# Tying every instruction of a planned decoder step to its written order on all five queues

## The chip, the cores and the metric

The kernel runs on one core of one Trainium2 chip. The core has five instruction queues: PE (TensorE, matrix multiplication; the profile shows its weight loads as PEld), DVE (VectorE), ACT (ScalarE), POOL (GpSimd) and SP (SyncE, which here issues all DMAs). Each queue is worked off in its order; an instruction that waits for a semaphore holds up what stands behind it. The metric is the device time of one execution in microseconds (us), the median of several runs. Lower is better.

## The reference

One layer of a hybrid decoder for 16 meta tokens, a prompt of 256 tokens and 8 x 4 sample tokens, 304 columns in all, in float32. Cut to what matters:

```
xn = rms_norm(x, norm_mix)
z = xn @ w_in                                  # 2048 -> 3360 + 4096 columns
o_a, S_a = rwkv7_mixer(z[:, :3360], ...)       # 16 heads of 64: a recurrence with state S
o_b, S_b = retention_mixer(z[:, 3360:], ...)   # 4 heads of 256: chunkwise retention
h = x + concat(o_a, o_b) @ w_out               # 2048 -> 2048
hn = rms_norm(h, norm_ffn)
h = h + (silu(hn @ w_gate) * (hn @ w_up)) @ w_down   # 2048 -> 5632 -> 2048
y = rms_norm(h, norm_final)
```

It returns y for prompt and samples, the last row of z of each sequence (the token shift), and the new states.

## The kernel before

**The main stream.** All weights lie in one array, `big`, in the order of their use: the input projection (59 tiles of up to 128 columns), the output projection in two halves of 16 tiles, and then, four hidden tiles at a time, gate, up and down. `main` (L608) walks through it. A weight is wanted as the sum of two float32r parts, so for every 512 columns, called a half here, ACT casts the raw weights to `wh` (`cast`, L591) and DVE takes the rest into `wl` (`rest`, L603). The activations are split in the same way into `xh` and `xl`. Each step of `main` issues three matmuls into an accumulator `acc`: wh by xh, wh by xl, wl by xh. Raw weights come in loads of 1024 columns, 512 KB, into one of four buffers `wr` (`load`, L582); `wh` and `wl` have four buffers each (`WS = 4`), `acc` has two banks of PSUM, and the other six banks serve the small matmuls (tag `mm`). At the start of a half, `main` writes loads up to four chunks of 1024 columns ahead, and casts so that the half two places on is cast; `rest` for that one is written in the middle of the half:

```
while self.loaded < min(total, at + WR * WCOLS):
    self.load()
while self.halved < min(total, at + (1 if starting else WS - 1) * 512):
    self.cast()
...
if o == 256:
    self.rest()
```

**The streams.** All other work is written as generators, called streams here: the evacuation of an accumulator (`evacuate`, L653), the eight pairs of RWKV heads (`pair`, L880, with `by_token`, `inverse`, `units`, `sample` and `pair_out`), the four retention heads (`ret`, L1353), norms and gates. A stream issues some instructions and yields. `inverse` (L1069) has a chain on POOL: three groups of ten small operations, each behind five shuffles on DVE that bring its factors; the ten operations of a group and the five shuffles of the next are written together, and then the stream yields. `ret` loads the samples' states, `s0r`, in four transfers of 512 KB, two at a time. `prep` in `out_jobs` (L1593) splits eight tiles of the mixers' output at once (an ACT copy and a DVE subtraction for each), before each half of the output projection. `hn` (L673) does the same for the input of the feed-forward part; at the last tile of the output projection eight of them are written in a row. `need` of a job holds `main` back until what it reads has been issued.

**The order of the work.** The program is built twice. The first build is a draft in a throw-away program. There each instruction goes through `Timed` (L289) to `Plan.book` (L345), which keeps a clock for each engine and works out, from the places in memory that an instruction reads and writes and from written-in prices, when it starts and when its result can be used. `Plan.run` (L438) lets `main` go on by one step, or a stream whose time has come: `pick` (L421) takes the first stream, by rank, whose last instructions are all done by PE's clock, and `step` (L430) lets it issue up to its next yield and sets its time to the end of these plus 100 ns. Each choice is put into `log`. Then `Room.place` (L469) lays the tiles of the draft out in one arena per data type, two tiles in one place where their uses in the written order don't meet. The second build takes its choices from `log` and makes the same instructions in the same order. Outputs are kept in `self.outs` and are written to the program at least 20 us of PE's clock later (`put`, L539; `flush`, L543). The last statements of `build` (L1671) are the write of the token shift, `out_sh`, and a last flush:

```
self.plan.run(self.main(jobs))
self.sp.dma_start(self.O["sh"], self.shout)
self.flush(all=True)
```

**What happens to that order.** The second build runs in a `TileContext`. It finds which instruction depends on which, adds the semaphores, and puts the instructions of each engine into an order of its own; the order in which they were written is for it a rank among those that it takes to be ready. So in the kernel before, the written order is a wish and not what stands in the queues.

## Time and profile before

| | us |
|---|---|
| median of 3 runs | 1605.94 |
| lowest and highest | 1604.27, 1607.81 |
| the profiled execution | 1606.78 |
| its span, from the first to the last instruction | 1605.0 |

The rows of the profile are from the one profiled execution. Nearly every instruction carries L300, the line of `call` in `Timed`, so groups are told apart by their tiles: `acc<-xh,wl` is a matmul of `main` that reads the rest of a weight, `wh<-wr` a cast, `mm<-...` a small matmul of a stream, and `arena_dt.float` any tile of the float32 arena. A group's row has its number of instructions, busy time, mean duration of one in ns, and then the idle time of its engine before it with what ended that. A row of the waits has who waited for whom, us in total, times, and the longest. A row of the timeline has start and duration in us, and in brackets the idle time before it and what ended it. A row of the windows has the length of the stretch, busy us (and instructions) of PE, PEld, DVE, ACT and POOL, the granted clock of PE as a share of full, the share of DMA time, and GB/s. The stages by their tiles: the input projection with the mixers beside it to some 640 us, the output projection after it, the feed-forward part to some 1590 us, and the last norm.

### The profile page before, as it was taken

The page shows a single profiled execution, that of the slowest core. Times are in us where ns is not written, and L with a number is a line of the kernel's source. Part 1 is how long each engine was busy: PE and PEld are TensorE (multiplying, and loading weights), DVE is VectorE, ACT ScalarE, POOL GpSimd, SP SyncE. Part 2 cuts the span into 40 slices and gives each one's busy share as a digit, 9 for nine tenths or more (in the row PEclk, how much of TensorE's full clock was granted, in tenths as well). Part 3 has the DMA queues.
Part 4 walks back from the last instruction along what each step waited for, and adds up shares of the span by engine and source line. Part 5 has one row for each costly group of instructions (what it writes and reads, how often), then busy time and mean ns, then how long its engine had stood idle before and what let it go on. Part 6 is the DMA issues. An engine that isn't in the chain of part 4 may idle for free.

```text
span 1605.0 us, 31012 instructions
## 1 busy us (share of the span) xinstructions
PE 1552.0 (97%) x11388; PEld 1518.1 (95%) x11388; DVE 1125.4 (70%) x2590; ACT 841.2 (52%) x1795; POOL 186.5 (12%) x567
## 2 busy tenths in 40 slices
PE   9998899988998999999999999999999999999997
PEld 8988898887997899999999999999999999999997
DVE  7988778886897759767565656565666666565657
ACT  6756676746775565456444444444444444444445
POOL 1454323422141300000000000000000000000000
PEclk9999999999999999999999999999999999999998
DMA  8443333334445347755555555555555555555553
GB/s 278 147 126 99 106 111 113 110 114 147 140 139 172 91 154 239 239 166 161 168 162 167 171 161 169 170 162 168 168 163 169 166 164 170 164 165 171 163 167 112
DMA packets 77001, 252.50 MB, mean 157 GB/s; under 512 B 9393, under 2 KB 14641, under 8 KB 76849
## 3 DMA queue, kind: packets, MB, share of 16 engines
q1 hardware_dynamic: 76848, 250.52, 50.4%
q8 instruction: 90, 1.47, 0.4%
q14 instruction: 63, 0.51, 0.1%
HBM read 236.21 MB, written 14.28 MB: 156 GB/s over the span
## 4 chain that ended last, share of the span: by engine, by line
PE 66%; DVE 1%; ACT 0%; issue 0%; POOL 0%; DVEq 0%; POOLq 0%
PE acc L300 63%; PE mm L300 3%; DVE arena_dt.float L300 1%; ACT arena_dt.float L300 0%; DVE wl L300 0%; POOL arena_dt.float L300 0%; DVEq L1740 0%; ACT wh L300 0%; DVEq L300 0%; POOLq L300 0%
## 5 line engine op out<-in xcount | busy, mean ns | idle before, releaser
L300 ACT CAST wh<-wr 128x512 fp32r<-128x512 f32 x826 | 510.4, 620 | 585.6 <-PE acc L300 549.8
L300 PE MATMUL acc<-xh,wh 128*128 128x288 f32 (+2 forms) x2592 | 793.3, 306 | 0.0
L300 PE MATMUL acc<-xh,wl 128*128 128x288 f32 (+2 forms) x2592 | 773.7, 299 | 6.5 <-DVE wl L300 6.5
L300 PE MATMUL acc<-xl,wh 128*128 128x288 f32 (+2 forms) x2592 | 770.9, 297 | 0.0
L300 DVE TENSOR_TENSOR wl<-wr,wh 128x512 fp32r<-128x512 f32 x826 | 570.5, 692 | 280.0 <-ACT wh L300 256.5
L300 PEld LDWEIGHTS acc<-xh,wl 128*128 128x128 f32 x2592 | 489.5, 189 | 8.7 <-DVE wl L300 7.2
L300 PEld LDWEIGHTS acc<-xh,wh 128*128 128x128 f32 x2592 | 491.0, 189 | 4.9 <-issue 1.9
L300 PEld LDWEIGHTS acc<-xl,wh 128*128 128x128 f32 x2592 | 490.0, 189 | 3.5 <-issue 0.2
L300 PE MATMUL acc<-arena_dt.float32r,wh 128*128 128x288 f32 x1408 | 279.9, 294 | 0.0
L300 PEld LDWEIGHTS acc<-arena_dt.float32r,wh 128*128 128x128 f32 x1408 | 226.3, 188 | 0.3 <-ACT arena_dt.float32r L300 0.3
L300 PE MATMUL acc<-arena_dt.float32r,wl 128*128 128x288 f32 x704 | 207.9, 295 | 0.0
L300 PE MATMUL mm<-arena_dt.float 128*128 128x128 f32 (+6 forms) x1072 | 175.3, 320 | 31.5 <-DVE arena_dt.float L300 13.3
L300 PEld LDWEIGHTS mm<-arena_dt.float 128*128 128x128 f32 (+1 forms) x1072 | 141.6, 185 | 48.3 <-issue 18.8
L300 DVE TENSOR_TENSOR arena_dt.float<-arena_dt.float 128x288 f32<-128x288 f32 (+11 forms) x483 | 158.0, 354 | 11.7 <-ACT arena_dt.float L300 6.2
L300 DVE TENSOR_TENSOR arena_dt.float<-arena_dt.float,acc 128x288 f32<-128x288 f32 x208 | 94.3, 454 | 64.2 <-PE acc L300 64.1
L300 PEld LDWEIGHTS acc<-arena_dt.float32r,wl 128*128 128x128 f32 x704 | 132.3, 188 | 0.0
L300 ACT COPY arena_dt.float<-mm 64x64 f32<-64x64 f32 (+9 forms) x330 | 91.8, 287 | 57.9 <-PE mm L300 52.3
L300 ACT ACTIVATE arena_dt.float<-arena_dt.float 128x288 f32<-128x288 f32 (+6 forms) x200 | 85.5, 432 | 49.5 <-DVE arena_dt.float L300 37.7
L300 DVE TENSOR_TENSOR arena_dt.float<-acc,arena_dt.float 128x288 f32<-128x288 f32 (+4 forms) x181 | 72.9, 420 | 31.3 <-PE acc L300 30.5
L300 POOL TENSOR_TENSOR arena_dt.float<-arena_dt.float 128x75 f32<-128x75 f32 (+14 forms) x240 | 81.4, 339 | 61.1 <-DVE arena_dt.float L300 36.7
L300 POOL COPY arena_dt.float<-arena_dt.float 128x32 f32<-128x32 f32 (+4 forms) x123 | 45.3, 384 | 102.0 <-DVE arena_dt.float L300 49.4
L300 POOL MEMSET arena_dt.float<- 128x64 f32 (+8 forms) x137 | 30.9, 238 | 184.4 <-DVE arena_dt.float L300 82.3
(64 smaller groups left out, 693.3 us busy)
## 6 DMA issues: line engine op xcount, KB each, us to landing
wr<-big SPq DMA_DIRECT2D x409, 512.0 KB, 3.5
arena_dt.float<-s0r SPq DMA_DIRECT2D x16, 512.0 KB, 4.6
out_rts<-arena_dt.float SPq DMA_DIRECT2D x16, 512.0 KB, 2.8
arena_dt.float<-xT SPq DMA_DIRECT2D x4, 576.0 KB, 4.7
out_y<-arena_dt.float SPq DMA_DIRECT2D x8, 288.0 KB, 2.2
arena_dt.float<-xT SPq DMA_DIRECT2D x7, 304.0 KB, 5.6
wr<-big SPq DMA_DIRECT2D x8, 256.0 KB, 5.5
arena_dt.float<-lora SPq DMA_DIRECT2D x16, 128.0 KB, 2.3
```

The costliest lines, as they stand in the source:

```text
L300: return f(*a, **k)
```

## The change

The kernel hands `Plan` a function `keep`. In the second build it is `tc.keep_in_program_order`, in the draft it does nothing. `Timed` passes each instruction through it. For an instruction it looks for the one written last on the same engine and adds an edge between the two that fixes their order in the queue and adds no semaphore. As each engine of the kernel is reached through `Timed`, and SP's DMAs too, all five queues then hold their instructions in the order in which they were written.

```diff
@@ class Timed
         def call(*a, **k):
             self._plan.book(self._name, what, a, k)
-            return f(*a, **k)
+            return self._plan.keep(f(*a, **k))
@@ class Plan
-    def __init__(self, nc, rooms, draft, log):
+    def __init__(self, nc, rooms, draft, log, keep):
+        self.keep = keep
         self.rooms, self.draft, self.log, self.count = rooms, draft, log, 0
@@ class Step
-        self.plan = pl = Plan(self.nc, rooms, draft, log)
+        self.plan = pl = Plan(self.nc, rooms, draft, log, (lambda i: i) if draft else tc.keep_in_program_order)
```

## The prediction

> **What bounds the kernel now.** I read the page first: shares, then slices.

> ```profile
> span 1605.0 us, 31012 instructions
> PE 1552.0 (97%) x11388; PEld 1518.1 (95%) x11388; DVE 1125.4 (70%) x2590; ACT 841.2 (52%) x1795; POOL 186.5 (12%) x567
> PE   9998899988998999999999999999999999999997
> DVE  7988778886897759767565656565666666565657
> ```

> PE is the bound, and each slice is 40.1 us, so all the eights lie in the first 13, before 525 us. The windows view by stage says how much is open:

> ```profile
> core 0: us, PE busy (x) PEld busy (x) DVE busy (x) ACT busy (x) POOL busy (x), PEclk, DMA share, GB/s
> 60.00:600.00 540.00, 499.92 (x3506) 472.12 (x3505) 426.62 (x1326) 342.25 (x906) 171.38 (x515) 0.97 0.41 125
> 600.00:640.00 40.00, 40.00 (x283) 39.24 (x283) 37.81 (x85) 22.16 (x47) 0.00 (x0) 1.00 0.70 231
> 640.00:1580.00 940.00, 939.97 (x7104) 937.57 (x7104) 594.79 (x1038) 424.81 (x741) 0.00 (x0) 1.00 0.55 169
> 1580.00:1605.00 25.00, 14.51 (x110) 14.07 (x108) 16.66 (x37) 9.62 (x19) 0.00 (x0) 0.78 0.24 95
> ```

> From 640 us on PE is never idle, its clock is full, and 7104 matmuls in 939.97 us are 132 ns each: no order can shorten that. What can move lies in 60 to 600: 540 - 499.92 = 40.1 us idle, and a granted clock of 0.97, worth 0.03 x 540 = 16 us. The pot is 56 us. The waits view of PE for that stretch says who ends the idle time (39.6 us together):

> ```profile
> PE mm L300 <- DVE arena_dt.float L300: 13.3, 7, 4.7
> PE mm L300 <- ACT arena_dt.float L300: 11.1, 12, 3.9
> PE mm L300 <- DMA arena_dt.float<-s0r: 8.7, 3, 6.8
> PE acc L300 <- DVE wl L300: 6.5, 3, 3.3
> ```

> These are few, long waits at the head of PE's queue. To see what an order has to do with them I took two in the timeline. The first is the wait for wl at 91 us (PE, then DVE, then POOL):

> ```profile
> 94.45 0.41 PE L300 MATMUL acc<-xh,wl 128*128 128x304 f32 x1 [3.28 <-DVE wl L300]
> ...
> 89.63 0.01 DVE L300 LOAD_MASK_SELECT arena_dt.float<-arena_dt.float  x1 [2.10 <-POOL arena_dt.float L300]
> 91.73 0.01 DVE L300 LOAD_MASK_SELECT arena_dt.float<-arena_dt.float  x1 [0.43 <-POOL arena_dt.float L300]
> 93.69 0.71 DVE L300 TENSOR_TENSOR wl<-wr,wh 128x512 fp32r<-128x512 f32 x1
> ...
> 85.17 10.87 POOL L300 TENSOR_TENSOR arena_dt.float<-arena_dt.float 128x75 f32<-128x75 f32 x26
> ```

> POOL is in the chain of `inverse`. DVE stands with a shuffle at its head, waiting for POOL, and the wl that PE needs is queued behind it. The second is the longest wait, 6.8 us for s0r (SP, POOL, PE):

> ```profile
> 480.59 0.34 SPq L300 DMA_DIRECT2D out_sh<-shout  x1
> 481.02 0.89 SPq L300 DMA_DIRECT2D arena_dt.float<-s0r  x2
> ...
> 480.00 0.56 POOL L300 COPY shout<-arena_dt.float 128x1 f32<-128x1 f32 x2
> ...
> 487.07 2.04 PE L300 MATMUL mm<-arena_dt.float 128*32 128x256 f32 x16 [6.79 <-DMA arena_dt.float<-s0r]
> ```

> The write of out_sh is the last but one statement of build, yet here it goes at 480.6 us. SP issued it as soon as POOL's copies into shout were through, with two loads of s0r right behind it, and PE waited for one of these. So today's order isn't the order of the code, and it puts instructions ahead of their inputs on in-order queues.

> **The change, part by part.** It adds no arithmetic, no transfer and no semaphore wait of its own: each instruction is tied behind the one written before it on its engine. What moves is the order on PE, DVE, ACT, POOL and SP. The written order is made by the draft: `pick` lets a stream go on when the draft's PE clock has reached the end of all that the stream last issued. So it is as good as the draft's prices. I check these against rows:

> ```profile
> L300 ACT CAST wh<-wr 128x512 fp32r<-128x512 f32 x826 | 510.4, 620 | 585.6 <-PE acc L300 549.8
> L300 DVE TENSOR_TENSOR wl<-wr,wh 128x512 fp32r<-128x512 f32 x826 | 570.5, 692 | 280.0 <-ACT wh L300 256.5
> wr<-big SPq DMA_DIRECT2D x409, 512.0 KB, 3.5
> arena_dt.float<-s0r SPq DMA_DIRECT2D x16, 512.0 KB, 4.6
> ```

> Cast: 108 + 0.83 x 512 + 94 = 627 ns against 620. Rest: 62 + 1.05 x 512 + 83 = 683 against 692. Matmul of 288 columns: 0.417 x 288 + 13 = 133 against 132. POOL at 75 elements: 260 + 2.4 x 75 = 440, and 60 + 30 more where one needs the other's output, against 10.87 / 26 = 418. A 512 KB load: 1.4 + 1.64 + 0.6 = 3.6 us against 3.5 for wr and 4.6 for s0r. The prices hold within a few per cent, are long on POOL and 1 us short on s0r. So:

> 1. PE's waits for DVE and ACT, 24.4 us. A small matmul is written where its inputs are due, with weight matmuls ahead of it. An input late by 0.2 us costs 0.2 us, not 4. I leave 5 of 24.4: -19.4. Bounds: 0 left, or all 24.4.
> 2. Wait for s0r, 8.7 us. out_sh goes to the end, and the long one of 6.8 goes; the other 1.9 stays, as s0r is priced short: -6.8.
> 3. Wait for wl, 6.5 us. In the written order DVE gets the second and third group of shuffles only when POOL's ten operations before are due, so it doesn't stand before POOL: -6.5.
> 4. **What comes back.** The cast of half h+2 is written at the start of half h, its rest in the middle of half h, 1.5 halves = 18 matmuls = 2.4 us before its use. With 0.69 for the operation itself, 1.7 us are left; now a cast may run until its four buffers are full. A burst over 1.7 us on DVE, or one over 2 us on ACT, then reaches PE, since casts and rests are queued behind it. Three bursts are plain in the code: twice eight copies and rests in `prep`, and the eight `hn` at the last out tile. This row gives 0.40 us for one:

> ```profile
> 84.32 0.80 ACT L300 ACTIVATE arena_dt.float<-arena_dt.float 128x288 f32<-128x288 f32 x2
> ```

>    Eight are 3.2 us, the lead of a cast is two halves, 3.2 us, and then come the cast and the rest, 1.3 us: 1.3 to 1.5 us of PE each, 4 in all. Smaller pile-ups, where two pairs, a sample and an evacuation come at once, I put at 0.5 us for each of 8 pairs and 4 heads, 6 us. Together +10. Bounds: 0, and the second rival's 65.
> 5. Clock. 16 us are lost after waits. These rows are of the stretches behind the wait at 94.45 and behind two more, whose rows stand below them:

> ```profile
> 94.00:100.00 6.00, 5.54 (x29) 5.55 (x30) 6.00 (x16) 1.97 (x4) 3.56 (x10) 0.72 0.29 105
> 347.00:353.00 6.00, 5.16 (x27) 4.85 (x27) 2.53 (x5) 2.27 (x7) 0.56 (x2) 0.72 0.24 87
> 379.00:385.00 6.00, 4.70 (x34) 4.47 (x35) 5.56 (x16) 2.73 (x7) 0.38 (x1) 1.00 0.55 155
> ...
> 347.84 1.64 PE L300 MATMUL mm<-arena_dt.float 128*128 128x128 f32 x8 [2.25 <-DVE arena_dt.float L300]
> 379.65 0.41 PE L300 MATMUL acc<-xh,wl 128*128 128x304 f32 x1 [2.41 <-DVE wl L300]
> ```

>    The first two fall to 0.72, the third doesn't, so two waits of one length cost different amounts, and I scale with idle time: 39.6 - 32.7 + 10 = 17 us left of 40, thus 7 of 16 us: -9. [...]
> 6. The end. out_sh now stands behind the eight writes of y: one more issue, +0.5 us. The first 20 us and all from 640 to 1580 I cost at nothing: there PE is fed by casts and rests alone, DVE is 63% busy (594.79 / 940), and the 1.7 us above cover one evacuation. If that cover fails, rival two decides.

> Sum: -19.4 - 6.8 - 6.5 + 10 - 9 + 0.5 = -31. The profiled execution took 1606.8 us (span 1605.0 and 1.8 around it), so it becomes 1575.6; the median before, 1605.9, is 0.8 lower: **1575**.

> [...]

> **Rivals.**
> - **Only what is plainly out of order pays.** The draft is slower than the chip at each hand-over: a stream waits 100 ns and then for the next group of three matmuls, 0.4 us. Then the chains of the pairs lag, `need` blocks the main stream, and PE waits as long elsewhere. For: POOL's price is long. Against: almost every long wait now has weight matmuls right behind it, so PE had work. Only out_sh's 6.8 us and its stretch at half clock, 3.4 us, go: 1606 - 10 = 1596.
> - **Slower: casts late.** In the strict order every wait of DVE at the head of its queue passes to the rest behind it. The waits view for 60 to 600:

> ```profile
> DVE arena_dt.float L300 <- PE mm L300: 41.4, 38, 6.1
> DVE arena_dt.float L300 <- POOL arena_dt.float L300: 28.5, 30, 3.1
> DVE wl L300 <- ACT wh L300: 23.4, 27, 3.2
> ```

>   If those for PE and for casts reach PE whole, that is 65 us on 1565 (the forecast without its 10): 1630. It decides once the rests are late by 0.18 us a half on average (41 us of gain over some 230 halves before 640 us: of 826 halves, 12 matmuls or 1.59 us each, 940 / 1.59 come later). For: DVE is at 426.62 / 540 = 79% there, and at 95% in 600 to 640. Against: only 3 waits of PE for wl today, though DVE stands waiting that long.
> - **Nothing moves.** If the order were already that of the code: 1606. out_sh speaks against it.

> **How the numbers follow.** Forecast 1575, chance 0.64; its own range is 1557 (the pot but for 7 us) to 1594 (the new waits at 29 instead of 10). Only what is out of order, 1596: 0.14. Casts late, 1612 to 1650: 0.15. Nothing: 0.04. Better than 1557: 0.03. For eight in ten the range goes from 1556 to 1608. 0.2% is 3.2 us, about what a measurement of this kernel can tell from no change: faster 0.78, same 0.06, slower 0.16.

> **What would show it.** PE's waits for DVE and ACT in the stretch to 600 fall under 10 us, that for s0r under 3; out_sh is issued after the last y; shuffles no longer wait one by one for POOL; the granted clock there is 0.98 or more. PE's waits for wl are more in number and short, the longest near `prep` and `hn`. Wrong if PE idles anywhere from 750 to 1580, if wl waits go over 20 us, or if SP holds loads of wr behind a load that waits for its place in the arena.

## The result, and the profile after

| | before | after |
|---|---|---|
| median of 5 runs, us | 1605.09 | 1595.29 |
| lowest and highest, us | 1604.27, 1607.81 | 1593.34, 1598.29 |
| the profiled execution and its span, us | 1606.78, 1605.0 | 1595.29, 1593.5 |

The ratio is 0.9937, 95% interval 0.9922 to 0.9953: faster by 0.6%, 10 us, where 31 were forecast. The sign was right, and the time lies in the wide range (1556 to 1608), but 1 us outside the forecast's own (1557 to 1594): it is the time of the first rival (1596), not that of the forecast (1575).

The windows view of the kernel after, with the columns of before:

```profile
core 0: us, PE busy (x) PEld busy (x) DVE busy (x) ACT busy (x) POOL busy (x), PEclk, DMA share, GB/s
20.00:60.00 40.00, 38.87 (x279) 36.85 (x278) 33.75 (x74) 24.93 (x50) 9.07 (x25) 1.00 0.54 169
60.00:600.00 540.00, 510.10 (x3615) 476.96 (x3614) 446.24 (x1364) 344.75 (x924) 156.94 (x537) 1.00 0.42 129
600.00:640.00 40.00, 39.50 (x295) 37.29 (x294) 27.31 (x60) 20.44 (x44) 0.00 (x0) 1.00 0.77 261
640.00:1580.00 940.00, 938.40 (x7087) 937.17 (x7085) 575.16 (x1054) 417.14 (x751) 0.00 (x0) 1.00 0.55 167
```

In 60 to 600 us the granted clock is 1.00 instead of 0.97: nearly the whole loss by the clock is gone. PE's idle time fell from 40.1 to 29.9 us, not to the 17 of the forecast. It is other idle time than before, as the waits view of PE for the same stretch shows (us in total, times, longest):

```profile
PE acc L300 <- DVE wl L300: 11.4, 18, 1.2
PE mm L300 <- ACT arena_dt.float L300: 6.8, 8, 1.7
PE mm L300 <- POOL arena_dt.float L300: 4.6, 4, 1.6
PE mm L300 <- DVE arena_dt.float L300: 2.0, 4, 1.2
PE mm L300 <- DMA arena_dt.float<-s0r: 1.9, 4, 0.9
PE mm L300 <- issue: 1.8, 2, 1.3
```

No wait is over 1.7 us any more, where there were waits of 3.3 to 6.8. But there are six times as many before DVE's rests: 18 instead of 3.

These two views promise 10 us of idle time and 16 of clock, and only 11.5 us of span came. The rest hides in how idle time is counted. A record of a matmul of the main stream is about 300 ns long (297 to 306 ns on average on the page of before), while the next one starts after 132 (939.97 us for 7104 of them from 640 to 1580 us), so by these two numbers a wait shows as idle time only beyond some 0.17 us. I therefore took the starts of all matmuls from both traces, and for each the distance to the next less the lower quartile of that distance for the same pair of tiles in all traces of this study. An excess of 0.3 us or more is a wait, one in a stretch at half clock counts as clock, and smaller ones are put together:

```
us, first to last matmul             before   after
undisturbed distances                1460.1   1459.5
waits of matmuls of the main stream     8.8     22.0
waits of small matmuls                 38.2     25.8
half clock                             18.3      1.6
distances longer by under 0.3 us       69.1     73.1
```

So 12.4 us of waits before small matmuls went, 13.2 us of waits in the main stream came, and the small delays grew by 4. How the pairs are told apart moves the rows: with the shapes of the two matmuls counted too, the main stream's waits go from 7.4 to 19.0 us, those of small matmuls from 39.3 to 26.6 and the half clock from 16.8 to 2.1, and the changes agree with the table's within some 2 us. **In the sum, PE waits about as long as before (47.0 and 47.8 us); what the change gained is the clock**, because the waiting now falls so that it leaves the clock nearly alone: one stretch at half clock in 60 to 600 us, where there were seven (see the last section).

### The profile page after: what moved, and what is told of

Read it like the earlier page. It is cut to its first block, busy times and chain, and to the rows that moved or that the text cites. A ratio compares the mean times of both kernels' runs of the same rounds, so it can differ in the third digit from the quotient of the medians.

```text
span 1593.5 us, 30795 instructions
## 1 busy us (share of the span) xinstructions
PE 1547.0 (97%) x11388; PEld 1506.5 (95%) x11388; DVE 1101.9 (69%) x2590; ACT 822.2 (52%) x1795; POOL 166.5 (10%) x567
## 4 chain that ended last, share of the span: by engine, by line
PE 71%; DVE 6%; DMA 2%; ACT 1%; issue 1%; POOL 1%; DVEq 0%; POOLq 0%; ACTq 0%; SPq 0%
PE acc L300 66%; PE mm L300 5%; DVE arena_dt.float L300 5%; DVE wl L300 1%; ACT arena_dt.float L300 1%; DMA arena_dt.float<-s0r 1%; POOL arena_dt.float L300 1%; DMA arena_dt.float<-lora 1%; DVE arena_dt.float32r L300 0%; ACT wh L300 0%; DVE xl L300 0%; ACT arena_dt.float32r L300 0%; DVEq L1741 0%; POOL shout L300 0%; POOLq L300 0%
## 5 line engine op out<-in xcount | busy, mean ns | idle before, releaser
L300 PE MATMUL acc<-xh,wh 128*128 128x288 f32 (+2 forms) x2592 | 791.7, 305 | 0.6 <-ACT wh L300 0.6
L300 PE MATMUL acc<-xh,wl 128*128 128x288 f32 (+2 forms) x2592 | 772.8, 298 | 13.3 <-DVE wl L300 13.2
L300 PE MATMUL acc<-xl,wh 128*128 128x288 f32 (+2 forms) x2592 | 766.8, 296 | 0.0
L300 ACT CAST wh<-wr 128x512 fp32r<-128x512 f32 x826 | 500.9, 617 | 363.8 <-PE acc L300 327.7
L300 DVE TENSOR_TENSOR wl<-wr,wh 128x512 fp32r<-128x512 f32 x826 | 562.8, 689 | 127.8 <-ACT wh L300 124.8
L300 PEld LDWEIGHTS acc<-xh,wl 128*128 128x128 f32 x2592 | 486.1, 188 | 19.7 <-DVE wl L300 18.9
L300 PEld LDWEIGHTS acc<-xh,wh 128*128 128x128 f32 x2592 | 487.8, 188 | 5.9 <-issue 1.3
L300 PEld LDWEIGHTS acc<-xl,wh 128*128 128x128 f32 x2592 | 486.9, 188 | 3.7 <-issue 0.5
L300 PE MATMUL acc<-arena_dt.float32r,wh 128*128 128x288 f32 x1408 | 280.0, 294 | 0.4 <-ACT arena_dt.float32r L300 0.3
L300 PEld LDWEIGHTS acc<-arena_dt.float32r,wh 128*128 128x128 f32 x1408 | 226.3, 188 | 0.9 <-ACT arena_dt.float32r L300 0.6
L300 PE MATMUL acc<-arena_dt.float32r,wl 128*128 128x288 f32 x704 | 208.0, 295 | 0.0
L300 DVE TENSOR_TENSOR arena_dt.float<-acc,arena_dt.float 128x288 f32<-128x288 f32 (+4 forms) x181 | 72.8, 420 | 167.1 <-PE acc L300 166.2
L300 PE MATMUL mm<-arena_dt.float 128*128 128x128 f32 (+6 forms) x1072 | 172.0, 311 | 15.4 <-ACT arena_dt.float L300 5.9
L300 PEld LDWEIGHTS mm<-arena_dt.float 128*128 128x128 f32 (+1 forms) x1072 | 138.1, 181 | 32.7 <-ACT arena_dt.float L300 8.5
L300 DVE TENSOR_TENSOR arena_dt.float<-arena_dt.float 128x288 f32<-128x288 f32 (+10 forms) x483 | 158.5, 355 | 10.8 <-ACT arena_dt.float L300 4.3
L300 DVE TENSOR_TENSOR arena_dt.float<-arena_dt.float,acc 128x288 f32<-128x288 f32 x208 | 94.4, 454 | 100.4 <-PE acc L300 99.9
L300 ACT ACTIVATE arena_dt.float<-arena_dt.float 128x288 f32<-128x288 f32 (+6 forms) x200 | 85.2, 433 | 122.7 <-DVE arena_dt.float L300 115.5
L300 ACT COPY arena_dt.float<-mm 64x64 f32<-64x64 f32 (+11 forms) x330 | 91.7, 286 | 80.6 <-PE mm L300 74.9
L300 PEld LDWEIGHTS acc<-arena_dt.float32r,wl 128*128 128x128 f32 x704 | 132.4, 188 | 0.0
L300 ACT CAST arena_dt.float32r<-arena_dt.float 128x288 fp32r<-128x288 f32 (+4 forms) x73 | 30.4, 423 | 124.2 <-DVE arena_dt.float L300 92.6
L300 POOL TENSOR_TENSOR arena_dt.float<-arena_dt.float 128x75 f32<-128x75 f32 (+14 forms) x240 | 86.9, 362 | 73.1 <-DVE arena_dt.float L300 50.1
L300 POOL MEMSET arena_dt.float<- 128x64 f32 (+8 forms) x137 | 29.7, 238 | 181.3 <-DVE arena_dt.float L300 102.9
## 6 DMA issues: line engine op xcount, KB each, us to landing
wr<-big SPq DMA_DIRECT2D x409, 512.0 KB, 3.6
arena_dt.float<-s0r SPq DMA_DIRECT2D x16, 512.0 KB, 5.1
out_rts<-arena_dt.float SPq DMA_DIRECT2D x16, 512.0 KB, 5.6
```

Source lines behind the costliest of these rows:

```text
L300: return self._plan.keep(f(*a, **k))
```

## The experiments

All were timed beside the kernel before on the same chip. The first column of figures is the median in us, with that of before in the same call; waits and clock are of 60 to 600 us, idle time as the profile counts it. The long lead is the run lead3, the short one that of the kernel before and of the change.

| run | queues tied | lead of the cast | us (before) | ratio, 95% interval | PE waits for wl | PE's other waits | clock |
|---|---|---|---|---|---|---|---|
| pin_pe | PE | short | 1609.4 (1604.1) | 1.0031, 1.0017 to 1.0045 | 6.6 | 37.0 | 0.97 |
| pin_sp | SP | short | 1601.3 (1604.1) | 0.9985, 0.9971 to 0.9999 | 3.8 | 32.1 | 0.98 |
| pin_act | ACT | short | 1601.0 (1607.8) | 0.9963, 0.9948 to 0.9978 | 9.2 | 24.3 | 0.97 |
| pin_dve | DVE | short | 1584.2 (1604.5) | 0.9885, 0.9859 to 0.9911 | 7.9 | 11.3 | 1.00 |
| pin_dap | DVE, ACT, POOL | short | 1587.2 (1604.1) | 0.9887, 0.9865 to 0.9910 | 9.6 | 9.9 | 1.00 |
| all_but_pe | all but PE | short | 1590.8 (1604.7) | 0.9916, 0.9890 to 0.9941 | 10.3 | 8.6 | 1.00 |
| all_but_sp | all but SP | short | 1592.9 (1604.7) | 0.9930, 0.9908 to 0.9952 | 9.4 | 19.1 | 0.99 |
| margin300 | all | short | 1606.3 (1604.5) | 1.0016, 1.0000 to 1.0033 | 9.7 | 26.9 | 0.98 |
| rest0 | all | rest earlier | 1581.0 (1604.5) | 0.9860, 0.9835 to 0.9885 | 3.2 | 9.0 | 1.00 |
| **lead3** | all | long | **1569.4** (1604.1) | 0.9777, 0.9751 to 0.9802 | 1.7 | 12.4 | 1.00 |
| lead3_margin | all | long | 1569.9 (1604.5) | 0.9793, 0.9772 to 0.9815 | 1.2 | 14.0 | 1.00 |
| lead3_dap | DVE, ACT, POOL | long | 1573.8 (1604.7) | 0.9813, 0.9792 to 0.9835 | 1.7 | 15.2 | 0.99 |
| lead3_dve | DVE | long | 1583.9 (1607.8) | 0.9856, 0.9841 to 0.9871 | 3.7 | 20.8 | 0.98 |
| lead3_free | none | long | 1592.0 (1604.7) | 0.9927, 0.9901 to 0.9953 | 5.6 | 28.2 | 0.98 |

### Which queue's order matters

Each variant ties some engines only, here PE:

```diff
-        self.plan = pl = Plan(self.nc, rooms, draft, log, (lambda i: i) if draft else tc.keep_in_program_order)
+        self.plan = pl = Plan(self.nc, rooms, draft, log, (lambda i: i) if draft else
+                              (lambda i: tc.keep_in_program_order(i) if i.ins.engine in (mybir.EngineType.PE,) else i))
```

PE alone:

> The kernel before with PE's queue alone tied to the written order. Theory A (the long waits come from the order on DVE, ACT and POOL; PE's own order hardly moved): PE's waits and the granted clock stay as before, 1603 to 1608 us. Theory B (PE's order was the fault, as the prediction had it: small matmuls ahead of their inputs): most of the change's 10 us are here already, 1593 to 1599.

Measured 1609: theory A, 1 us above its range, and slower than before by 0.3%. The two programs, laid side by side queue by queue, say why. PE's queue hardly differs between the kernel before and the one after; DVE's, ACT's and POOL's do (an instruction that moved counts as two lines, where it left and where it came to):

```
queue   instructions   lines of difference
PE             10770                   112
DVE             2470                  1820
ACT             1793                   876
POOL             567                   368
SP               523                   138
```

PE's small matmuls stood ahead of their inputs in both; their place in PE's queue was not the fault, the lateness of the inputs was.

SP alone (`mybir.EngineType.SP` in the tuple):

> The kernel before with SP's queue alone tied. Theory A: only the wait behind the write of out_sh goes, 6.8 us, with some 3 us of half clock behind it, so 1595 to 1599 at best; the waits for wl and for DVE and ACT stay. Theory C (only what is plainly out of order pays, the first rival of the prediction): the same 1595 to 1599, and then nothing is left for the other queues: DVE, ACT and POOL tied alone give 1603 to 1608.

Measured 1601, ratio 0.9985: out_sh goes to the end, but a wait for s0r of 5.3 us stays in the profile:

```profile
PE mm L300 <- DMA arena_dt.float<-s0r: 5.7, 2, 5.3
```

The transfer that the prediction saw held up by out_sh comes late for another reason too. What is plainly out of order on SP pays 3 us, not 10.

DVE, ACT and POOL:

> DVE, ACT and POOL tied, PE and SP left free. Theory A: the waits of over 2 us for DVE, ACT and wl fall apart into many short ones, the clock in 60 to 600 us goes to 0.99 or more but for the stretch behind out_sh, PE's waits for wl double to 10 us or more, and the time is 1594 to 1600. Theory C: 1603 to 1608.

Measured 1587, better than expected and better than the change itself; the clock is 1.00. So the gain comes from these three. To part them:

> The kernel before with DVE's queue alone tied. If the long waits come from DVE standing at its head before POOL's chain (28.5 us in 60 to 600 before): these waits fall under 15 us, the granted clock there goes from 0.97 to 0.99 or more, and the time to 1590 to 1598. If ACT's order, or all three together, make the long waits: clock 0.97 to 0.98 and 1600 to 1608.

> The kernel before with ACT's queue alone tied. Theory E: DVE still stands before POOL (over 20 us in 60 to 600), the waits of over 2 us and the half clock stay (granted clock 0.97 to 0.98), casts are written late for it, 1602 to 1612. Theory F: ACT's order carries a part of the gain, clock 0.985 or more, 1592 to 1600.

DVE alone gives 20 us, 1584, better than either theory's time, and 1.00. ACT alone gives 7 us, at a clock of 0.97. Two rows of the waits view, first of the kernel with ACT tied, then of the one with DVE tied, show DVE before POOL:

```profile
DVE arena_dt.float L300 <- POOL arena_dt.float L300: 21.2, 24, 4.1
```

```profile
DVE arena_dt.float L300 <- POOL arena_dt.float L300: 14.1, 13, 4.0
```

Before it was 28.5 us in 30 waits, and with all five tied it is:

```profile
DVE arena_dt.float L300 <- POOL arena_dt.float L300: 10.5, 10, 3.4
```

The halving with DVE tied agrees with DVE no longer being given shuffles one by one while POOL works, though the longest single wait did not shrink (4.1 and 4.0, before 3.1). For ACT neither theory fits whole: the time lies between the two, the clock (0.97) and DVE's waits for POOL (21.2 us) are those of the first, and still its order is worth 7 us.

With all five tied, about half of what DVE alone gains is given back. Two runs were to say by which queue:

> The changed kernel with SP's queue left free. With DVE, ACT and POOL tied alone the time was 1587, with all five 1595: one of the two other queues costs some 8 us. Theory A: it is SP; in the written order the loads of lora stand behind loads of wr that wait for their buffer, and ACT stands before lora (29.7 us in 60 to 600 with all five, 11.6 without PE and SP). Then this gives 1584 to 1590, and ACT's waits for lora are under 15 us. Theory B: it is PE; then this gives 1592 to 1597.

> The changed kernel with PE's queue left free. Theory A (SP's order costs the 8 us): 1592 to 1597, ACT's waits for lora stay over 25 us. Theory B (PE's order costs them): 1584 to 1590.

Neither theory holds. With SP free ACT waits 10.9 us for lora instead of 29.7, as A had it, but the time is 1593; with PE free ACT still waits 29.4 us, and the time is 1591. The steps from 1584 over 1587 and 1591 to 1595 are each about as large as the intervals (by the ratios DVE alone and DVE with ACT and POOL are the same, 0.9885 and 0.9887, and tying PE or SP beside these three gives 0.9930 and 0.9916), and no single queue was found.

### The lead of casts and rests

The waits for wl in the kernel after, taken back through the timeline. At 106 us (SP, ACT, DVE, PE):

```profile
97.17 3.79 SPq L300 DMA_DIRECT2D wr<-big  x2
101.02 0.42 SPq L300 DMA_DIRECT2D arena_dt.float<-lora  x1
...
104.44 0.41 ACT L300 CAST arena_dt.float32r<-arena_dt.float 128x256 fp32r<-128x256 f32 x1 [5.07 <-DMA arena_dt.float<-lora]
104.75 0.62 ACT L300 CAST wh<-wr 128x512 fp32r<-128x512 f32 x1
...
105.70 0.69 DVE L300 TENSOR_TENSOR wl<-wr,wh 128x512 fp32r<-128x512 f32 x1
...
106.44 0.40 PE L300 MATMUL acc<-xh,wl 128*128 128x290 f32 x1 [0.49 <-DVE wl L300]
```

SP issues two loads of wr, the second only when its buffer is free (SP's own waits there show 3.1 us for a rest, wl); lora stands behind them. ACT stands before lora for 5.07 us with casts of wh queued behind. Then cast and rest run in a row, and PE waits. The buffer of wr is free when casts and rests have read it: so a late rest makes the next load late, and that can make the next cast late. At 741 us, behind the eight `hn`, the burst that the prediction named (ACT, DVE, PE):

```profile
735.84 3.09 ACT L300 ACTIVATE xh<-arena_dt.float,pv 128x288 fp32r<-128x288 f32 x7
739.17 2.17 ACT L300 CAST wh<-wr 128x512 fp32r<-128x512 f32 x4
...
737.57 3.51 DVE L300 SCALAR_TENSOR_TENSOR xl<-arena_dt.float,pv,xh 128x288 fp32r<-128x288 f32 x8
741.00 1.29 DVE L300 TENSOR_TENSOR wl<-wr,wh 128x512 fp32r<-128x512 f32 x2
...
741.74 0.40 PE L300 MATMUL acc<-xh,wl 128*128 128x288 f32 x1 [1.12 <-DVE wl L300]
```

The second picture is the common one. After 40 us, 20 matmuls of the main stream wait for wl. At 14 of them the cast of that half had ended more than 2 us before its rest began, so the rest was late on DVE and not for want of the cast. In the 4 us before the rest DVE had been busy for 95% or more at 10 of the 20, and had stood before POOL at 6, before ACT at 3 and before PE at 1. ACT had stood before lora in the 6 us before the cast at only two, those at 64.5 and 106.4 us.

The first test gives the cast, and with it the rest, one half more:

```diff
-                while self.halved < min(total, at + (1 if starting else WS - 1) * 512):
+                while self.halved < min(total, at + (1 if starting else WS) * 512):
```

> The changed kernel with the cast written three halves ahead of its use instead of two (WS in place of WS - 1), so the rest has 2.5 halves, 4.0 us, instead of 2.4. If the short lead makes PE wait for wl (11.4 us of idle time in 60 to 600, some 20 us counted from start to start of the matmuls): those waits fall under 4 us and the time to 1578 to 1588. If casts and rests are late because ACT and DVE are held up for longer than any lead (ACT stands before the loads of lora for up to 5.2 us): wl waits stay over 8 us and the time within 3 us of 1595.

Measured 1569.4: 26 us under the change, better than the first theory's 1578 to 1588, and the fastest kernel of this study. The waits view of PE for 60 to 600 us:

```profile
PE mm L300 <- ACT arena_dt.float L300: 5.9, 8, 2.7
PE mm L300 <- POOL arena_dt.float L300: 2.9, 1, 2.9
PE mm L300 <- issue: 2.0, 2, 1.7
PE acc L300 <- DVE wl L300: 1.7, 1, 1.7
```

wl has gone from 18 waits to one. ACT's waits for lora went with it, though nothing was done about them; this is the row of ACT in 60 to 600 with the short lead, and then with the long one:

```profile
ACT arena_dt.float32r L300 <- DMA arena_dt.float<-lora: 29.7, 10, 5.2
```

```profile
ACT arena_dt.float32r L300 <- DMA arena_dt.float<-lora: 10.9, 5, 4.6
```

That agrees with the one half of the circle described above, from late rests to late loads. The other half, from lora to PE's waits for wl, carries little: with SP free (all_but_sp) ACT also waits 10.9 us for lora, and PE still 9.4 us for wl. Counted from start to start, the waits of the main stream fell from 22.0 to 5.3 us and those of small matmuls from 25.8 to 18.0: 24.5 of the 26 us.

The rest alone half a half earlier, the cast as it was:

```diff
-                if self.rests and self.rests[0][0] is lo:
-                    self.rest()
-            if o == 256:
                 self.rest()
```

> The changed kernel with the rest written at the start of a half, beside the cast, instead of in its middle: 2.0 halves of lead for DVE instead of 1.5, the cast's lead unchanged. If it is the rest that is written too late on DVE: PE's waits for wl fall from 11.4 us of idle time in 60 to 600 to under 6, 1582 to 1590. If it is the cast on ACT, whose lead is the same: they stay over 9, 1592 to 1598.

Measured 1581, with 3.2 us of waits for wl in 60 to 600. So the rest was written too late. But this run loses in the feed-forward part, where the change lost nothing. There evacuations on DVE come late for PE. The rest is now written right behind its cast, but why that costs here is not shown: DVE stands before casts (wl for wh) for 203.5 us in the stretch below, and in lead3 for 192.1 us without a loss. Windows from 780 to 1540 us, rest0 first and then lead3, and between them what PE waits for in rest0:

```profile
780.00:1540.00 760.00, 755.99 (x5656) 753.88 (x5655) 460.58 (x787) 314.03 (x547) 0.00 (x0) 1.00 0.53 164
```

```profile
PE acc L300 <- DVE arena_dt.float L300: 4.0, 10, 0.4
```

```profile
780.00:1540.00 760.00, 759.60 (x5746) 759.15 (x5745) 472.56 (x809) 337.07 (x573) 0.00 (x0) 1.00 0.54 166
```

In the same 760 us rest0 gets 90 matmuls fewer done, 12 us at 132 ns.

Is the long lead a gain of its own?

> The kernel before, with no queue tied, and the cast written three halves ahead. Theory A (the lead matters where the order is tied; a free order already runs casts to the end of their four buffers, as ACT's 549.8 us of waits for PE show): 1599 to 1608, long waits and half clock as before. Theory D (the longer lead is a gain of its own, tied or not): 1585 or less.

Measured 1592.0, between the two theories: the lead gives 13 us with no queue tied, though casts there already ran ahead of the written order. Tying all five gives 10 us at the short lead, and 23 at the long one (1592 to 1569). Both together give 35, more than the 23 of the two added. Whether DVE's order is enough then:

> The cast three halves ahead and DVE alone tied. With the short lead DVE alone gave 1584 and all five 1595. Theory E (the order of DVE is what pays, and tying the others costs only where casts and rests are short of time): with the long lead the others cost nothing, so this is within 4 us of the 1569 of all five, 1565 to 1573. Theory F (the order of ACT is a gain of its own once the lead is long): this stays at 1576 to 1584.

> The cast three halves ahead, DVE, ACT and POOL tied, PE and SP free. If the loss by SP's order and the short lead are two things, the gains add: 1569 - 8 = 1561 or less. If late casts and rests were what held wr's buffers, and so SP and lora (ACT waits 11 us for lora in 60 to 600 with the long lead and all five tied), little is left to gain: 1566 to 1572.

With DVE alone tied 1584: theory F. PE now waits longer for ACT: the row is of lead3_dve in 60 to 600 us, against 5.9 us in 8 waits above. That points to ACT's free order, though POOL, PE and SP are free here too:

```profile
PE mm L300 <- ACT arena_dt.float L300: 14.5, 12, 4.3
```

With DVE, ACT and POOL tied it is 1574, near the second theory: where the lead is long, freeing SP and PE has nothing to give and loses some 4 us.

### The hand-over in the draft

```diff
-        self.end = max(self.end, done + 100)
+        self.end = max(self.end, done + 300)
```

> The changed kernel with the draft's hand-over made longer: a stream goes on 300 ns after the end of its last instructions instead of 100. Theory M (small matmuls wait because the draft's prices are a little short, so each input is late by some tenths of a us): PE's waits before small matmuls fall to under half (18 us of idle time in 60 to 600 to under 9), 1580 to 1588 us. Theory N (inputs are late because ACT and DVE are held up, before lora, by pile-ups and by late casts, for longer than a margin covers; the longer hand-over only slows the chains): these waits stay over 14 us, 1590 to 1602.

> The long lead of the cast (1569 us) with the longer hand-over. Theory M: 1557 to 1564. Theory N: 1566 to 1576.

At the short lead 1606, worse than either theory had it. PE's waits for ACT before small matmuls rose from 6.8 to 19.9 us, and the clock fell to 0.98; why was not followed further. At the long lead nothing changes, 1569.9: theory N. So 200 ns more of hand-over don't cover what makes the inputs late.

## Why the prediction was right or wrong

Measured from start to start of the matmuls, so that each term can be held against its own:

| step | forecast, us | measured, us |
|---|---|---|
| 1 and 2: waits of small matmuls | -26.2 | -12.4 |
| 3 and 4: waits for wl (of the main stream) | +3.5 | +13.2 |
| 5: clock | -9 | -16.7 |
| 6: out_sh at the end | +0.5 | +0.6 |
| distances longer by under 0.3 us | 0 | +4.0 |
| sum | -31 | -11.3 |

- **Step 1 failed in its mechanism.** "A small matmul is written where its inputs are due, with weight matmuls ahead of it": PE's queue held the small matmuls at nearly these places already (112 lines of difference in 10770 instructions), and tying it alone gives nothing (1609). What made the inputs late was DVE's order and, less, ACT's (1584 and 1601 tied alone). In idle time the waits for DVE, ACT, POOL and issue fell from 24.4 to 16.1 us, not to 5. I took a matmul that waits at the head of its queue for a matmul put there too early, and didn't ask whether its input was late.
- **Step 2** was right in size, 8.7 to 1.9 us, but out_sh was only one of its causes: with SP alone tied a wait of 5.3 us stays.
- **Step 3** was right in the main: DVE's waits for POOL fell from 28.5 us in 30 waits to 10.5 in 10, and PE's waits of 2.4 and 3.3 us for wl behind them are gone. But single waits of 3.4 and 2.7 us for POOL are left, with waits of 0.7 and 1.1 us of PE for wl behind them.
- **Step 4 had the right place and half of the size.** The lead of 2.4 us for a rest was read from the code, and lead3 and rest0 show that the lead is the cause. But the bursts came to 10 us where 22 us of waits came. Of the three that were named only that of `hn` made PE wait (1.12 us, 1.3 to 1.5 forecast); behind the eight copies and rests of `prep`, at 618 and 683 us, PE has no wait for wl. The size is in the smaller pile-ups: 12 of 0.5 us were forecast, and 18 waits with 11.4 us of idle time came in 60 to 600. As counted above, DVE was busy throughout before half of these waits, and stood before POOL ahead of six more. The circle over wr's buffers, SP and lora, by which lateness could feed itself, was in no term either, but it stands behind only two of the waits. In the rival of late casts the direction was right; its price of 65 us was far too high.
- **Step 5** was too careful. I scaled the clock's loss with idle time, and it went nearly whole (18.3 to 1.6 us) while the waiting stayed (47.0 and 47.8 us). What stood ahead of a half clock in these traces was mostly a piece of 3.41 us with much idle time in it, 1.78 us or more in 50 of 54 cases, as the last section shows. That this term gave 8 us more than forecast hid a part of what steps 1 and 4 missed.
- **Delays under 0.3 us** had no term in the sum and took 4 us; their cause was not looked for.
- **Step 6** was right: the last small group of matmuls starts at 1594.4 before and 1582.3 after, with 10.6 and 11.2 us from there to the end of the span.
- **The rivals.** The first gave the right time by luck, for a wrong reason: SP alone is worth 3 us of its 10. The margin run speaks for its mechanism, chains that lag when the hand-over gets longer, but at the draft's own value nothing shows that. That "nothing moves" was out.

What stays open: which of ACT, POOL, PE and SP costs what of the 10 us between DVE tied alone and all five tied at the short lead. Each step lies near the uncertainty.

## What to carry to other kernels

When an engine waits at the head of its queue, compare the order of its own queue with the order you mean to give it before you blame that order; the late input may come from another queue's order. When you fix the order of in-order queues, try a longer lead of the work that feeds the bound engine in the same step: here tying all five queues and the longer lead were worth 10 and 13 us alone, and 35 together. And price waits by where they fall and not by their sum alone: about the same 47 us of waiting cost 18.3 us of clock before the change and 1.6 after it.

## What the runs showed of the hardware

```profile
344.88:348.29 3.41, 1.16 (x10) 0.94 (x9) 3.34 (x8) 2.08 (x5) 1.00 (x4) 1.00 0.16 48
348.29:351.71 3.42, 3.42 (x16) 3.13 (x14) 0.89 (x3) 2.09 (x7) 0.25 (x1) 0.50 0.41 153
375.60:379.01 3.41, 1.64 (x12) 1.39 (x10) 0.51 (x2) 3.34 (x9) 2.17 (x10) 1.00 0.12 38
379.01:382.43 3.42, 2.72 (x19) 2.49 (x19) 3.36 (x9) 0.48 (x2) 0.00 (x0) 1.00 0.19 28
```

```profile
405.05:408.46 3.41, 1.59 (x7) 1.05 (x7) 2.84 (x8) 3.05 (x7) 0.21 (x1) 1.00 0.00 0
408.46:411.87 3.41, 3.41 (x14) 3.12 (x13) 2.25 (x6) 0.86 (x3) 0.00 (x0) 0.50 0.75 184
```

```profile
416.54:419.95 3.41, 1.97 (x16) 1.73 (x14) 3.17 (x8) 1.21 (x3) 0.77 (x2) 1.00 0.27 92
419.95:423.36 3.41, 2.17 (x17) 2.18 (x18) 2.45 (x7) 2.15 (x6) 0.04 (x1) 1.00 0.96 254
423.36:426.78 3.42, 3.42 (x29) 3.42 (x28) 2.96 (x6) 2.01 (x5) 0.20 (x1) 1.00 0.99 404
```

The pieces in which PE was busy for 1.16 and 1.59 us were followed by one at half clock; after those with 1.64, 1.97 and 2.17 us the clock stayed at 1.00. The wait of 2.68 us straddles an edge of the grid, so no piece holds more than 1.44 us of it. Over all 16 traces, from 20 to 1570 us, 54 pieces at full clock were followed by one at half. In 50 of them PE was idle by its records for 1.78 us or more, in the other four for 1.12 to 1.67 us; why these four turned is not known. None of the 7134 pieces followed by full clock has more than 1.77 us idle. In 60 to 600 us, 7 pieces turned before the change (1.89 to 3.41 us idle) and 1 after (1.82 us).
